# The compression MLP of a sparse-attention branch, moved between the projections of a delta rule and spread over four column quarters of TensorE

## The chip, the core and the metric

The kernel runs on one core of a Trainium2 chip. It is one program with five in-order engines: TensorE (PE, and PEld for its weight loads), VectorE (DVE), ScalarE (ACT), GpSimd (POOL) and SyncE (SP), whose queue issues nearly all transfers. The metric is device time in microseconds. Before the change three runs gave 2414.8, 2419.28 and 2424.24 us, so the median is 2419.28 us.

## The reference

One decoder layer on 256 tokens of width 2048: SwiGLU, a mixer with two branches, a second SwiGLU, final RMSNorm. The change concerns the mixer. One input projection feeds a gated delta rule with 8 heads of 128 and a sparse attention whose keys and values are also compressed: 15 blocks of 32 tokens (stride 16) for each of 2 key/value groups, so 30 positions, each flattened to 4096 numbers and put through a small MLP. It is done once for keys and once for values:

```python
def _compress(x, pos, w1, b1, w2):
    b, s, g, d = x.shape
    r = CMP_BLOCK // CMP_STRIDE
    n_cmp = s // CMP_STRIDE - r + 1
    xs = x.reshape(b, s // CMP_STRIDE, CMP_STRIDE, g, d)
    blocks = jnp.concatenate([xs[:, j:j + n_cmp] for j in range(r)], axis=2)
    blocks = blocks + pos[None, None, :, None, :]
    flat = blocks.transpose(0, 1, 3, 2, 4).reshape(b, n_cmp, g, CMP_BLOCK * d)
    return jax.nn.silu(flat @ w1 + b1) @ w2
...
    kc, vc, ks, vs, kw, vw = [t.reshape(b, s, NSA_KV_HEADS, NSA_HEAD_DIM) for t in jnp.split(nkv, 6, axis=-1)]
...
    kcmp = _compress(kc, pos_k, k_w1, k_b1, k_w2)
    vcmp = _compress(vc, pos_v, v_w1, v_b1, v_w2)
```

The attention's first step (`compressed`, L989) needs `kcmp`; the delta rule needs nothing of it.

## The kernel before

A projection is `win(c)` (L608): 128 output columns for all 256 tokens. Its weights come as two blocks of 128 x 1024 floats (512 KB) into the ring `raw` of six slots (`wload`, L157). ScalarE rounds a block to `whi` (L171), VectorE makes the rest `wlo` (L172), three buffers each, and TensorE then does 16 pairs of matmuls (`product`, L181 and L183). `both` (L207, L210) empties the bank. After each projection `ada(tk())` may put in a unit that streams two 512 KB blocks of `ada_w` through the same ring and adds them up on VectorE (L234); `paces` gives 4 units to the first 27 projections of the mixer and then one to each of the next 20. Every eighth unit ends in transposes (L240).

The delta rule runs in four groups of two heads (the loop of L913 to L918): `gdn_qkv` projects and convolves q, k and v of the next two heads while `gdn_group` works on the last two; its chain of small matmuls on TensorE (L730 to L895, among them the 32 x 32 steps L803 and L813) waits in turn on VectorE and ScalarE. `gdn_out` adds two gate projections. A scheduler lays the recorded work out, engine by engine, in one fixed order, so what stands in a queue behind a waiting instruction waits too.

The compression follows the last group (L932 to L972). Four projections give `cat`. For keys (b = 0) and then values (b = 1), `G` holds the 30 positions for each of the 32 offsets (L946, one buffer), and 32 matmuls of 128 x 30 against 128 x 128 weights (L952) add up in one bank of the `mm` ring, all of them in TensorE's first 32 columns. In float32 each such matmul is two passes. The eight 512 KB blocks of `cw1` lie in the `raw` ring until TensorE has read them. A tail of bias, tanh (L955 to L958), transpose (L960), copy (L962) and a second small matmul (L966 or L970) gives `kcmp` and `vcmp`. `attend_in` (8 projections) and `attend` follow for each of the two groups.

Of the kernel before, what the change touches and what calls it, by code (L numbers as in the profile page):

```python
# [18 lines left out]
F32 = mybir.dt.float32  # L19
# [3 lines left out]
AF = mybir.ActivationFunctionType  # L23
OP = mybir.AluOpType
# [3 lines left out]
P = 128  # L28
S = 256
# [26 lines left out]
NB = 15  # L56
# [9 lines left out]
C_I32 = C_CMP + 32  # L66
# [41 lines left out]
def trunk(tc, a, out, stage=99, dbg=None):  # L108
    nc = tc.nc
    ctx = ExitStack()  # L110
    with ctx:
# [30 lines left out]
        V = {}  # L142
# [53 lines left out]
        def tmpc():  # L196
            return tmp("tc", 2)
# [53 lines left out]
        def ada(n):  # L251
            for _ in range(n):
                if ada_q:
                    ada_unit(*ada_q.pop(0))
# [349 lines left out]
        with ExitStack() as mx:  # L604
            mp = mx.enter_context(tc.tile_pool(name="mp", bufs=1))
            tk = paces((4, 31 - 2 * NE), (20, 20), (24, 36))

            def win(c):  # L608
                if c in done:
                    return done.pop(c)  # L610
                ps = proj(a["win"][c], hT)
                ada(tk())
                return ps

            def one(tag="q", bufs=12):
# [88 lines left out]
            def gdn_qkv(h0):  # L704
                q, k, v = [], [], []
                for lst, w0, c0 in ((k, W_GK, 8), (q, W_GQ, 0), (v, W_GV, 16)):
                    for h in (h0, h0 + 1):
                        lst.append(conv_silu(win(w0 + h), c0 + h))
                        if h0 == 0 and len(q) + len(k) + len(v) == SCA:
                            scalars()  # L710
                return q, k, v
# [188 lines left out]
            def gdn_out(h0, oT):  # L900
                for i in range(2):
                    h = h0 + i
                    zg = both(win(W_GZ + h))
                    th = tmp()
                    nc.scalar.activation(th, zg, AF.Tanh, scale=0.5)
                    sg = mp.tile([P, S], F32, tag="sg", name="sg", bufs=1)
                    nc.vector.scalar_tensor_tensor(sg, th, 1.0, zg, op0=OP.add, op1=OP.mult)
                    sv = sg.rearrange("p (a b) -> p a b", a=2)
                    nc.vector.tensor_mul(sv, sv, v4(oT)[:, :, i])
                    oA[h] = big("oA", 8, (P, 2, S), F32R)  # L910
                    split(oA[h], sg)

            qkv = gdn_qkv(0)  # L913
            for h0 in (0, 2, 4, 6):
                oT = gdn_group(h0, *qkv)
                if h0 < 6:
                    qkv = gdn_qkv(h0 + 2)
                gdn_out(h0, oT)  # L918

            def rope(x, o, pt, tr):
# [5 lines left out]
                nc.vector.tensor_mul(o[:32], x[:32], cf[:32, C_COS:C_COS + S])  # L928
                nc.vector.tensor_add(o[:32], o[:32], t[:32])
                return o  # L930

            cat = [mp.tile([P, 2, S], F32, tag="cat", name="cat", bufs=2) for _ in range(2)]  # L932
            for b in range(2):
                for g in range(2):
                    both(win(W_KV + 2 * b + g), cat[b][:, g])
            kcmp = mp.tile([P, 2 * NB], F32, name="kcmp")
            vcmp = mp.tile([16, 2, P], F32, name="vcmp")
            b1 = mp.tile([2 * NB, 2, P], F32, name="b1")
            nc.scalar.dma_start(b1, bass.AP(tensor=a["cb1"].tensor, offset=a["cb1"].offset,
                                            ap=[[0, 2 * NB], [P, 2], [1, P]]))  # L940
            for b in range(2):
                G = mp.tile([P, 32, 2, NB], F32, tag="G", name="G", bufs=1)
                for g in range(2):
                    src = cat[b][:, g]
                    blocks = bass.AP(tensor=src.tensor, offset=src.offset, ap=[list(src.ap[0]), [1, 32], [16, NB]])
                    nc.vector.tensor_add(G[:, :, g], blocks,  # L946
                                         V["pos"][:, 32 * b:32 * b + 32].unsqueeze(2).to_broadcast([P, 32, NB]))
                ph = mmtile()
                for q, (raw, n) in enumerate(wload(a["cw1"][b], 32)):
                    for j in range(n):  # L950
                        jj = 8 * q + j
                        nc.tensor.matmul(ph[:2 * NB, :P], G[:, jj].rearrange("p a b -> p (a b)"), raw[:, j],  # L952
                                         start=(jj == 0), stop=(jj == 31))
                hid = mp.tile([2 * NB, P], F32, tag="hid", name="hid", bufs=1)
                nc.vector.tensor_add(hid, ph[:2 * NB, :P], b1[:, b])  # L955
                th = tmpc()[:2 * NB, :P]
                nc.scalar.activation(th, hid, AF.Tanh, scale=0.5)
                nc.vector.scalar_tensor_tensor(hid, th, 1.0, hid, op0=OP.add, op1=OP.mult)  # L958
                pt = ftile()
                nc.tensor.transpose(pt[:, :2 * NB], hid, ident[:2 * NB, :2 * NB])  # L960
                hT2 = tmpc()[:, :2 * NB]
                nc.scalar.activation(hT2, pt[:, :2 * NB], AF.Copy, scale=0.5)  # L962
                w2 = V["w2"][:, b * P:(b + 1) * P]
                pc = ftile()
                if b == 0:
                    nc.tensor.matmul(pc[:, :2 * NB], w2, hT2, start=True, stop=True)  # L966
                    nc.vector.tensor_copy(kcmp, pc[:, :2 * NB])
                else:
                    for g in range(2):
                        nc.tensor.matmul(pc[:NB, g * P:(g + 1) * P], hT2[:, g * NB:(g + 1) * NB], w2,  # L970
                                         start=True, stop=True)
                    nc.vector.tensor_copy(vcmp[:NB], pc[:NB, :2 * P].rearrange("p (a b) -> p a b", a=2))  # L972

            PR = [("pr", 2), ("pr", 2), ("G", 1)]

# [184 lines left out]


VEC = [("ada_b", 144), ("n1", 16), ("nm", 16), ("n2", 16), ("nf", 16), ("conv", 96), ("alog", 1), ("dtb", 1),
       ("gnw", 1), ("pos", 64), ("w2", 256)]


def layout(i):
    f = lambda n: np.asarray(i[n])
    cols = lambda v: np.ascontiguousarray(v.reshape(-1, P).T)

    def tiles(w):  # L1170
        k, n = w.shape
        return np.ascontiguousarray(w.reshape(k // P, P, n // P, P).transpose(2, 1, 0, 3))

    o = {}
    o["xT"] = np.ascontiguousarray(f("x")[0].T.reshape(KT, P, S).transpose(1, 0, 2))
# [19 lines left out]
    v = {"ada_b": cols(f("ada_b")[0]), "n1": cols(f("ffn1_norm")[0]), "nm": cols(f("mix_norm")[0]),  # L1195
         "n2": cols(f("ffn2_norm")[0]), "nf": cols(f("final_norm")),
         "conv": f("gdn_conv_w")[0].reshape(24, P, 4).transpose(1, 0, 2).reshape(P, 96),
         "alog": row32(f("gdn_a_log")[0]), "dtb": row32(f("gdn_dt_bias")[0]),
         "gnw": f("gdn_norm_w")[0].reshape(P, 1),
         "pos": np.concatenate([f("cmp_pos_k")[0].T, f("cmp_pos_v")[0].T], axis=1),  # L1200
         "w2": np.concatenate([f("cmp_k_w2")[0], f("cmp_v_w2")[0]], axis=1)}
    o["vec"] = np.ascontiguousarray(np.concatenate([v[n] for n, _ in VEC], axis=1))
    o["cw1"] = np.ascontiguousarray(np.stack([f("cmp_k_w1")[0], f("cmp_v_w1")[0]]).reshape(2, 32, P, P)
                                    .transpose(0, 2, 1, 3))
    o["cb1"] = np.ascontiguousarray(np.stack([f("cmp_k_b1")[0], f("cmp_v_b1")[0]]))
    o["consts"] = float_consts()
    o["masks"] = block_masks()
    return o
# [17 lines left out]
```

## Time and profile before

| | us |
|---|---|
| median of three runs | 2419.28 |
| the profiled execution | 2422.17 |
| its span | 2420.4 |
| PE busy | 2349.7 |
| DVE busy | 1789.9 |
| ACT busy | 1130.5 |

The rows below come from that one execution, whose granted TensorE clock was 0.99 on the mean; 1.8 us of its time lie outside its span. Times in rows are microseconds from the start of the span. A PE row counts a matmul as busy until its modelled end, so rows that follow each other overlap, and the cost of one in a stream is the distance of its start from the next start. "[1.70 <-DVE hid L958]" is idle time of the engine before the row, and what ended it.

### The profile page before, as it was taken

Reading aid. Unit: us, or ns where it says so; the run is one execution under the profiler, and the core shown is the slowest. Engines: PE = TensorE matmul, PEld = TensorE weight load, DVE = VectorE, ACT = ScalarE, POOL = GpSimd, SP = SyncE. Lnnn points to the kernel's source line nnn. Section 1 sums busy time; section 2 is a strip of 40 time slices with the busy share of each in tenths; the row PEclk is TensorE's granted clock in tenths of the full one; section 3 lists DMA queues with packets and bytes.
Section 4 is the critical chain, followed back from the end, with each engine's and each line's share of the span. In section 5 each row is a group of like instructions: output and inputs, shape, how many; then the busy total and the mean of one; then the engine's idle time right before and its main releaser. Section 6 shows DMA issues by size and latency. Waiting matters only on the chain.

```text
span 2420.4 us, 39304 instructions
## 1 busy us (share of the span) xinstructions
PE 2349.7 (97%) x15308; PEld 2062.4 (85%) x15308; DVE 1789.9 (74%) x2641; ACT 1130.5 (47%) x1780; POOL 1.2 (0%) x6
## 2 busy tenths in 40 slices
PE   7999999999999999999999999999999999999997
PEld 6999988888888988887888878889888888888886
DVE  6899878778887887785887677878666666555555
ACT  3533544334444565543544444556444444344443
POOL 0000000000000000000000000000000000000000
PEclk7999999999999999999999999999999999999999
DMA  9998688888996644566776887576777776665663
GB/s 326 317 312 306 199 282 302 280 274 296 315 303 218 220 159 142 157 204 211 262 256 214 289 275 257 188 236 201 238 240 236 231 235 204 189 191 185 183 184 121
DMA packets 182872, 571.08 MB, mean 236 GB/s; under 512 B 18047, under 2 KB 18333, under 8 KB 182685
## 3 DMA queue, kind: packets, MB, share of 16 engines
q1 hardware_dynamic: 181920, 566.43, 71.5%
q8 instruction: 120, 1.97, 0.3%
q10 hardware_dynamic: 765, 2.14, 0.2%
q14 instruction: 67, 0.55, 0.1%
HBM read 564.30 MB, written 4.19 MB: 235 GB/s over the span
## 4 chain that ended last, share of the span: by engine, by line
PE 74%; DMA 11%; DVE 9%; issue 3%; ACT 1%; DVEq 0%; ACTq 0%; SPq 0%
PE mm L181 39%; PE mm L183 20%; DMA adaraw<-in_ada_w_dram 8%; PE mm L348 8%; DVE wlo L172 3%; DMA sada<-in_ada_w_dram 2%; PE c L348 2%; DVE acc L234 1%; DVE wlo L343 1%; DMA raw<-in_win_dram 1%; DVE sacc L443 1%; ACT whi L171 0%; PE f L240 0%; PE c L1026 0%; PE c L813 0%
## 5 line engine op out<-in xcount | busy, mean ns | idle before, releaser
L181 PE MATMUL mm<-hpair,whi 128*128 128x512 f32 x3536 | 1260.9, 398 | 1.1 <-ACT t L203 1.1
L172 DVE TENSOR_TENSOR wlo<-raw,whi 128x1024 fp32r<-128x1024 f32 (+1 forms) x666 | 793.0, 1196 | 350.9 <-ACT whi L171 349.3
L171 ACT ACTIVATE whi<-raw 128x1024 fp32r<-128x1024 f32 (+1 forms) x666 | 689.3, 1037 | 726.2 <-PE mm L181 420.9
L183 PE MATMUL mm<-hpair,wlo 128*128 128x256 f32 x3536 | 1004.7, 284 | 18.6 <-DVE wlo L172 18.4
L181 PEld LDWEIGHTS mm<-hpair,whi 128*128 128x128 f32 x3536 | 665.5, 188 | 160.1 <-issue 1.8
L183 PEld LDWEIGHTS mm<-hpair,wlo 128*128 128x128 f32 x3536 | 668.2, 189 | 30.3 <-DVE wlo L172 24.6
L181 PE MATMUL mm<-apair,whi 128*128 128x512 f32 x1408 | 497.7, 397 | 0.0
L183 PE MATMUL mm<-apair,wlo 128*128 128x256 f32 x1408 | 397.3, 282 | 5.5 <-DVE wlo L172 5.5
L234 DVE SCALAR_TENSOR_TENSOR acc<-adaraw,cact,acc 128x1024 f32<-128x1024 f32 x210 | 268.8, 1280 | 133.8 <-DMA adaraw<-in_ada_w_dram 132.8
L181 PEld LDWEIGHTS mm<-apair,whi 128*128 128x128 f32 x1408 | 264.3, 188 | 64.0
L183 PEld LDWEIGHTS mm<-apair,wlo 128*128 128x128 f32 x1408 | 265.4, 188 | 8.6 <-DVE wlo L172 8.4
L348 PE MATMUL mm<-hpair,whi 128*128 128x256 f32 x1472 | 265.7, 283 | 2.4 <-ACT hpair L309 1.8
L348 PEld LDWEIGHTS mm<-hpair,whi 128*128 128x128 f32 x1472 | 228.1, 190 | 3.0 <-ACT hpair L309 1.9
L348 PE MATMUL mm<-hpair,wlo 128*128 128x256 f32 x736 | 209.3, 285 | 1.4 <-DVE wlo L343 1.4
L342 ACT ACTIVATE whi<-raw 128x1024 fp32r<-128x1024 f32 x112 | 118.4, 1059 | 141.3 <-DMA raw<-in_w1gu_dram 56.4
L343 DVE TENSOR_TENSOR wlo<-raw,whi 128x1024 fp32r<-128x1024 f32 x112 | 136.5, 1222 | 30.2 <-ACT whi L342 30.1
L348 PEld LDWEIGHTS mm<-hpair,wlo 128*128 128x128 f32 x736 | 139.8, 190 | 2.6 <-DVE wlo L343 2.2
L207 ACT ACTIVATE t<-mm 128x256 f32<-128x256 f32 x237 | 86.9, 367 | 17.7 <-PE mm L183 17.6
L210 DVE TENSOR_TENSOR t<-mm,t 128x256 f32<-128x256 f32 x193 | 80.7, 418 | 2.5 <-ACT t L207 2.4
L443 DVE SCALAR_TENSOR_TENSOR sacc<-sada,cact,sacc 128x1024 f32<-128x1024 f32 x57 | 73.0, 1281 | 8.0 <-DMA sada<-in_ada_w_dram 7.3
L532 ACT ACTIVATE t<-t 128x256 f32<-128x256 f32 x63 | 26.3, 418 | 100.5 <-DVE t L210 100.2
L546 DVE SCALAR_TENSOR_TENSOR xT<-mm,g,xT 128x256 f32<-128x256 f32 x128 | 61.7, 482 | 7.7 <-PE mm L183 5.6
(373 smaller groups left out, 1586.7 us busy)
## 6 DMA issues: line engine op xcount, KB each, us to landing
adaraw<-in_ada_w_dram SPq DMA_DIRECT2D x224, 512.0 KB, 5.1
raw<-in_w2gu_dram SPq DMA_DIRECT2D x180, 512.0 KB, 4.7
raw<-in_w1gu_dram SPq DMA_DIRECT2D x176, 512.0 KB, 5.9
raw<-in_win_dram SPq DMA_DIRECT2D x158, 512.0 KB, 5.0
sada<-in_ada_w_dram SPq DMA_DIRECT2D x64, 512.0 KB, 6.4
raw<-in_w1d_dram SPq DMA_DIRECT2D x64, 512.0 KB, 4.6
raw<-in_w2d_dram SPq DMA_DIRECT2D x64, 512.0 KB, 3.5
raw<-in_wup_dram SPq DMA_DIRECT2D x32, 512.0 KB, 4.6
```

The costliest lines, as they stand in the source:

```text
L171: nc.scalar.activation(hi[:, :n], raw[:, :n], AF.Copy)
L172: nc.vector.tensor_sub(lo[:, :n], raw[:, :n], hi[:, :n])
L181: nc.tensor.matmul(ps[:, :], hi, pairs[k][:, :, :].rearrange("p a b -> p (a b)"), start=(k == 0), stop=False, skip_group_check=True)
L183: nc.tensor.matmul(ps[:, S:2 * S], lo, pairs[k][:, 0, :], start=False, stop=(k == n - 1), skip_group_check=True)
L207: nc.scalar.activation(t, ps[:, S:2 * S], AF.Copy)
L210: nc.vector.tensor_add(o, ps[:, :S], t)
L234: nc.vector.scalar_tensor_tensor(acc, raw, cact[:, kt:kt + 1], acc, op0=OP.mult, op1=OP.add)
L342: nc.scalar.activation(hi, raw, AF.Copy)
L343: nc.vector.tensor_sub(lo, raw, hi)
L348: nc.tensor.matmul(ps[:, w], l[:, w, k], h[:, r], start=(first and w == k == x == 0), stop=(last and k == kb - 1 and x == 2), skip_group_c ...
L443: nc.vector.scalar_tensor_tensor(acc, raw, c, acc, op0=OP.mult, op1=OP.add)
L546: nc.vector.scalar_tensor_tensor(xT[:, d], pd[:, j * S:(j + 1) * S], g05[:, d:d + 1], xT[:, d], op0=OP.mult, op1=OP.add)
```

## The change

`compress` is now a generator. It is made after the first two heads' q, k and v are projected, and each later `win` call of the delta rule takes one step of it: a `cat` projection, or one block of `cw1` with its 8 matmuls, or a tail. Seven steps for the keys and seven for the values make 14, and 26 `win` calls follow. `G` has 32 columns, the last two zero. Matmul j goes to the quarter j % 4 of the columns, into 32 partitions of its own in a bank `f`. The tail copies the 128 x 128 partial sums (`hs`), adds the four quarters by a matmul with four stacked identities (which also turns the result round), and takes the bias from a packed vector instead of a DMA of its own.

```diff
-            def win(c):
+            beside = []
+
+            def win(c, step=True):
                 if c in done:
                     return done.pop(c)
                 ps = proj(a["win"][c], hT)
                 ada(tk())
+                if step and beside:
+                    next(beside[0], None)
                 return ps
...
+            def compress():
+                for b in range(2):
+                    cat = mp.tile([P, 2, S], F32, tag="cat", name="cat", bufs=2)
+                    for g in range(2):
+                        both(win(W_KV + 2 * b + g, False), cat[:, g])
+                        yield
+                    G = mp.tile([P, 32, 32], F32, tag="G", name="G", bufs=1)
+                    nc.gpsimd.memset(G[:, :, 2 * NB:], 0.0)
+                    for g in range(2):
+                        src = cat[:, g]
...
+                        nc.vector.tensor_add(G[:, :, g * NB:(g + 1) * NB], blocks,
...
+                    ph = ftile()
+                    for r in range(4):
+                        (raw, _), = wload(a["cw1"][b][:, 8 * r:8 * r + 8], 8)
+                        for j in range(8):
+                            jj = 8 * r + j
+                            q = slice(32 * (j % 4), 32 * (j % 4) + 32)
+                            nc.tensor.matmul(ph[q, :P], G[:, jj], raw[:, j], start=(jj < 4), stop=(jj >= 28),
+                                             skip_group_check=True)
+                        yield
+                    hs = mp.tile([P, P], F32, tag="hs", name="hs", bufs=1)
+                    nc.scalar.activation(hs, ph[:, :P], AF.Copy)
+                    pt = ftile()
+                    nc.tensor.matmul(pt[:, :2 * NB], hs, cf[:, C_I32:C_I32 + 2 * NB], start=True, stop=True)
+                    hid = mp.tile([P, 2 * NB], F32, tag="hid", name="hid", bufs=1)
+                    nc.scalar.activation(hid, pt[:, :2 * NB], AF.Identity, bias=V["b1"][:, b:b + 1])
+                    th = tmpc()[:, :2 * NB]
+                    nc.scalar.activation(th, hid, AF.Tanh, scale=0.5)
+                    hT2 = tmpc()[:, :2 * NB]
+                    nc.vector.scalar_tensor_tensor(hT2, th, 1.0, hid, op0=OP.add, op1=OP.mult)
...
             qkv = gdn_qkv(0)
+            beside.append(compress())
             for h0 in (0, 2, 4, 6):
                 oT = gdn_group(h0, *qkv)
                 if h0 < 6:
                     qkv = gdn_qkv(h0 + 2)
                 gdn_out(h0, oT)
+            for _ in beside.pop():
+                pass
...
-            nc.scalar.dma_start(b1, bass.AP(tensor=a["cb1"].tensor, offset=a["cb1"].offset,
-                                            ap=[[0, 2 * NB], [P, 2], [1, P]]))
...
-                ph = mmtile()
-                for q, (raw, n) in enumerate(wload(a["cw1"][b], 32)):
-                    for j in range(n):
-                        jj = 8 * q + j
-                        nc.tensor.matmul(ph[:2 * NB, :P], G[:, jj].rearrange("p a b -> p (a b)"), raw[:, j],
-                                         start=(jj == 0), stop=(jj == 31))
...
```

On TensorE, at the end of the last group of heads, the order before was this (L952 are the compression's matmuls, L240 the transposes of an `ada` unit, L895 the end of the delta rule's chain, L960 and L966 the tail):

```order
L240 MATMUL f<-cf,acc 128x128 x4
L952 MATMUL mm<-raw,G 30x128 x6
L240 MATMUL f<-cf,acc 128x128 x4
L952 MATMUL mm<-raw,G 30x128 x10
L895 MATMUL c<-cf,o 128x128 x4
L952 MATMUL mm<-raw,G 30x128 x16
L960 MATMUL f<-cf,hid 128x30
L966 MATMUL f<-tc,vec 128x30
L952 MATMUL mm<-raw,G 30x128 x32
L181 MATMUL mm<-hpair,whi 128x512
```

All 64 matmuls stood here, with the tail of the keys directly between those of the keys and those of the values. Now they stand in eights; the first eight (L941, in the first group of heads, where L807, L817 and L837 are steps of the delta rule) are these:

```order
L181 MATMUL mm<-hpair,whi 128x512
L807 MATMUL c<-tb,N 32x32 x8
L183 MATMUL mm<-hpair,wlo 128x256
L181 MATMUL mm<-hpair,whi 128x512
L183 MATMUL mm<-hpair,wlo 128x256
L817 MATMUL c<-zc,q_9247 32x32
L941 MATMUL f<-raw,G 32x128
L817 MATMUL c<-zc,q_9247 32x32 x7
L941 MATMUL f<-raw,G 32x128 x7
L181 MATMUL mm<-hpair,whi 128x512
L183 MATMUL mm<-hpair,wlo 128x256
```

The other seven bursts are whole and have a projection's matmuls on both sides; the tail's L947 stands 32 matmuls behind its last burst, and L957 13 matmuls behind L947. On SP, whose queue issues the blocks, this stood before around the compression:

```order
L230 DMA adaraw<-in_ada_w_dram 128x1024 x2
L162 DMA raw<-in_cw_dram 128x1024 x8
L162 DMA raw<-in_win_dram 128x1024 x2
L230 DMA adaraw<-in_ada_w_dram 128x1024 x2
L162 DMA raw<-in_win_dram 128x1024 x2
```

and this stands now, in the first two groups of heads:

```order
L162 DMA raw<-in_win_dram 128x1024 x12
L162 DMA raw<-in_cw_dram 128x1024
L162 DMA raw<-in_win_dram 128x1024 x2
L230 DMA adaraw<-in_ada_w_dram 128x1024 x2
L162 DMA raw<-in_cw_dram 128x1024
L162 DMA raw<-in_win_dram 128x1024 x2
L162 DMA raw<-in_cw_dram 128x1024
L162 DMA raw<-in_win_dram 128x1024 x2
L162 DMA raw<-in_cw_dram 128x1024
```

The eight blocks no longer follow each other: at least two blocks of a projection lie between any two of them.

## Rows read from the trace of the kernel before

**Rows 1.** The page, part 1: busy time, share and instructions of each engine.

```profile
PE 2349.7 (97%) x15308; PEld 2062.4 (85%) x15308; DVE 1789.9 (74%) x2641; ACT 1130.5 (47%) x1780; POOL 1.2 (0%) x6
```

**Rows 2.** Windows: the four head groups, the stretch to attention, and one inside attention.

```profile
core 0: us, PE busy (x) PEld busy (x) DVE busy (x) ACT busy (x) POOL busy (x), PEclk, DMA share, GB/s
871.10:931.70 60.60, 59.45 (x623) 50.18 (x622) 50.49 (x124) 35.91 (x88) 0.00 (x0) 0.99 0.45 142
931.70:994.90 63.20, 62.35 (x638) 52.22 (x637) 50.73 (x119) 34.58 (x84) 0.00 (x0) 1.00 0.47 151
994.90:1061.40 66.50, 65.08 (x656) 54.92 (x655) 53.08 (x123) 36.51 (x93) 0.00 (x0) 1.00 0.53 166
1061.40:1111.90 50.50, 47.67 (x558) 39.39 (x557) 38.24 (x93) 17.37 (x38) 0.00 (x0) 1.00 0.55 178
1111.90:1180.80 68.90, 64.60 (x398) 54.73 (x396) 51.93 (x67) 26.12 (x39) 0.00 (x0) 0.98 0.87 299
...
1200.00:1220.00 20.00, 20.00 (x116) 16.53 (x115) 19.23 (x43) 11.04 (x30) 0.00 (x0) 1.00 0.71 231
```

**Rows 3.** Timeline (start, us, engine, line): a projection's pairs, first and eighth L181.

```profile
1085.60 0.39 PE L181 MATMUL mm<-hpair,whi 128*128 128x512 f32 x1
...
1088.05 0.40 PE L181 MATMUL mm<-hpair,whi 128*128 128x512 f32 x1
```

**Rows 4.** Groups by line, TensorE, 1100 to 1140: busy, mean ns, idle before.

```profile
L952 PE MATMUL mm<-raw,G 128*30 128x128 f32 x128 | 14.7, 273 | 0.0
...
L970 PE MATMUL f<-vec,tc 128*15 128x128 f32 x4 | 0.9, 364 | 0.9 <-ACT tc L962 0.9
...
L960 PE MATMUL f<-cf,hid 30*128 30x30 f32 x2 | 0.5, 228 | 3.1 <-DVE hid L958 3.1
L966 PE MATMUL f<-tc,vec 128*128 128x30 f32 x2 | 0.4, 284 | 0.3 <-ACT tc L962 0.3
```

**Rows 5.** Timeline: two runs of L952, the first with its entry wait.

```profile
1113.25 3.41 PEld L952 LDWEIGHTS mm<-raw,G 128*30 128x30 f32 x32 [0.17 <-issue]
...
1119.47 7.17 PE L952 MATMUL mm<-raw,G 128*30 128x128 f32 x64
```

**Rows 6.** Timeline: 32 x 32 steps on four tiles and on two.

```profile
1088.74 0.34 PEld L803 LDWEIGHTS c<-tb,N 32*32 32x32 f32 x32 [0.26 <-issue]
1088.74 0.45 PE L803 MATMUL c<-tb,N 32*32 32x32 f32 x32
...
1092.71 0.44 PE L803 MATMUL c<-tb,N 32*32 32x32 f32 x16
```

**Rows 7.** Groups by line, 845 to 1320, the same steps: busy, mean ns, idle before.

```profile
L803 PE MATMUL c<-tb,N 32*32 32x32 f32 x576 | 9.1, 194 | 4.4 <-DVE tb L794 4.4
```

**Rows 8.** Timeline: four pairs after the values' tail, first and fifth L181.

```profile
1132.84 0.80 PE L181 MATMUL mm<-hpair,whi 128*128 128x512 f32 x1
...
1135.57 0.44 PE L181 MATMUL mm<-hpair,whi 128*128 128x512 f32 x1
```

**Rows 9.** Windows: the tail of the values, and those four pairs.

```profile
1126.60:1132.80 6.20, 3.90 (x20) 2.59 (x19) 2.63 (x4) 1.45 (x3) 0.00 (x0) 0.95 0.89 347
1132.80:1135.60 2.80, 2.80 (x10) 2.38 (x10) 1.46 (x3) 1.06 (x1) 0.00 (x0) 0.50 1.00 377
```

**Rows 10.** Groups by line, VectorE, 845 to 1320: busy, mean ns, idle before.

```profile
L172 DVE TENSOR_TENSOR wlo<-raw,whi 128x1024 fp32r<-128x1024 f32 x112 | 136.1, 1219 | 30.7 <-ACT whi L171 30.0
L234 DVE SCALAR_TENSOR_TENSOR acc<-adaraw,cact,acc 128x1024 f32<-128x1024 f32 x56 | 71.4, 1274 | 9.9 <-DMA adaraw<-in_ada_w_dram 9.8
...
L946 DVE TENSOR_TENSOR G<-cat,vec 128x480 f32<-128x480 f32 x4 | 3.9, 972 | 0.0
```

**Rows 11.** Waits of SP's queue, 1060 to 1181: us, times, longest.

```profile
SPq L162 <- PE mm L952: 21.1, 5, 16.1
```

**Rows 12.** The page, part 6: transfers of a projection's weights, median to landing.

```profile
raw<-in_win_dram SPq DMA_DIRECT2D x158, 512.0 KB, 5.0
```

More of the change, by code (lines that the diff above doesn't have):

```diff
@@ L911, in gdn_out @@
                     split(oA[h], sg)
+            kcmp = mp.tile([P, 2 * NB], F32, name="kcmp")
+            vcmp = mp.tile([16, 2, P], F32, name="vcmp")
+            def compress():
[8 more added lines that the diff above has]
+                        src = cat[:, g]
+                        blocks = bass.AP(tensor=src.tensor, offset=src.offset, ap=[list(src.ap[0]), [1, 32], [16, NB]])
+                        nc.vector.tensor_add(G[:, :, g * NB:(g + 1) * NB], blocks,
+                                             V["pos"][:, 32 * b:32 * b + 32].unsqueeze(2).to_broadcast([P, 32, NB]))
+                    ph = ftile()
[17 more added lines that the diff above has]
+                    nc.vector.scalar_tensor_tensor(hT2, th, 1.0, hid, op0=OP.add, op1=OP.mult)
+                    w2 = V["w2"][:, b * P:(b + 1) * P]
+                    pc = ftile()
+                    if b == 0:
+                        nc.tensor.matmul(pc[:, :2 * NB], w2, hT2, start=True, stop=True)
+                        nc.scalar.activation(kcmp, pc[:, :2 * NB], AF.Copy, scale=0.5)
+                    else:
+                        for g in range(2):
+                            nc.tensor.matmul(pc[:NB, g * P:(g + 1) * P], hT2[:, g * NB:(g + 1) * NB], w2,
+                                             start=True, stop=True)
+                        nc.scalar.activation(vcmp[:NB], pc[:NB, :2 * P].rearrange("p (a b) -> p a b", a=2), AF.Copy,
+                                             scale=0.5)
+                    yield
@@ L930, in rope @@
                 return o
[L932 to L938, printed above, removed]
-            nc.scalar.dma_start(b1, bass.AP(tensor=a["cb1"].tensor, offset=a["cb1"].offset,
-                                            ap=[[0, 2 * NB], [P, 2], [1, P]]))
@@ L941, in trunk @@
[L941 to L947, printed above, removed]
-                ph = mmtile()
-                for q, (raw, n) in enumerate(wload(a["cw1"][b], 32)):
-                    for j in range(n):
-                        jj = 8 * q + j
-                        nc.tensor.matmul(ph[:2 * NB, :P], G[:, jj].rearrange("p a b -> p (a b)"), raw[:, j],
-                                         start=(jj == 0), stop=(jj == 31))
[L954 to L972, printed above, removed]
@@ L1162 @@
 VEC = [("ada_b", 144), ("n1", 16), ("nm", 16), ("n2", 16), ("nf", 16), ("conv", 96), ("alog", 1), ("dtb", 1),
-       ("gnw", 1), ("pos", 64), ("w2", 256)]
+       ("gnw", 1), ("pos", 64), ("w2", 256), ("b1", 2)]
 def layout(i):
@@ L1200, in layout @@
          "pos": np.concatenate([f("cmp_pos_k")[0].T, f("cmp_pos_v")[0].T], axis=1),
-         "w2": np.concatenate([f("cmp_k_w2")[0], f("cmp_v_w2")[0]], axis=1)}
+         "w2": np.concatenate([f("cmp_k_w2")[0], f("cmp_v_w2")[0]], axis=1),
+         "b1": np.stack([f("cmp_k_b1")[0], f("cmp_v_b1")[0]], axis=1)}
     o["vec"] = np.ascontiguousarray(np.concatenate([v[n] for n, _ in VEC], axis=1))
@@ L1204, in layout @@
                                     .transpose(0, 2, 1, 3))
-    o["cb1"] = np.ascontiguousarray(np.stack([f("cmp_k_b1")[0], f("cmp_v_b1")[0]]))
     o["consts"] = float_consts()
```

## Prediction

> **What bounds the kernel now.** I read the page's busy shares first. TensorE is busy 2349.7 us of 2420.4, every other engine 74% or less [rows 1]. So a change gains only what it takes out of TensorE's stream or its waits, and a delay costs only where it reaches that stream. Next come windows over the mixer, cut where VectorE starts each group of heads (871.1, 931.7, 994.9, 1061.4), where it ends the last (1111.9) and where attention starts (1180.8) [rows 2]. The reader is to see that TensorE is nearly full in the first three, that its gaps grow from 1061 on (2.8 and 4.3 us outside its busy time), and that VectorE stands at 75 to 83% throughout. The compression lies at the end, from 1108 to 1133. A projection's price is read from its pairs: seven in 2.45 us, 0.35 a pair, so 16 take 5.6 us [rows 3].
>
> **What is removed.** The 64 matmuls L952 are 128 passes and fill 14.7 us of TensorE with nothing beside them on that engine [rows 4]. In the longer run 64 passes take 7.17 us, the last of them 0.27, so one pass starts (7.17 - 0.27) / 63 = 0.11 us after the other [rows 4, 5]. A run begins with an entry wait of about 0.17 us [rows 5]; at four runs, as the order has them, I count three of these outside the busy time, 0.5, and put the whole at 15.2 us.
>
> Between the runs TensorE waits for the tails: 3.1 us at L960, 0.3 at L966 and 0.9 at L970, together 4.3 [rows 4]. These waits arise because the tail's links stand in TensorE's queue with few or no matmuls between them. The four pairs after the values' tail then take 2.73 us instead of 4 x 0.35 = 1.40, a loss of 1.3 [rows 3, 8]; the granted clock of that stretch is 0.50, so 1.2 GHz, behind 6.2 us in which TensorE was busy for 3.9 [rows 9]. Waits and slow pairs make 5.6 us. What is late next there is the projections and attention's first steps, which need nothing of the tails for eight projections more.
>
> **What is added.** The same 128 passes, now in eight bursts of 16, four streams of four passes each. The trace of before has no burst whose tiles share all rows and differ in columns alone, so the price is bounded from two sides. As one stream a burst takes 15 x 0.11 + 0.27 + 0.17 = 2.1 us, eight of them 16.7. Wholly side by side it takes 3 x 0.11 + 0.27 + 0.17 = 0.77, eight of them 6.2. The nearest rows are the delta rule's 32 x 32 steps: 32 passes on four tiles take 0.45 us, 16 passes on two tiles 0.44 [rows 6]. With 0.19 for the last one [rows 7] that is 8 ns from start to start on four tiles and 17 on two: twice the tiles, half the distance. Those tiles differ in rows and columns both. I take 6.2, since it is the only behaviour that any row of side-by-side tiles shows, and the upper end stays in the range. TensorE then gains 15.2 - 6.2 = 9.0 us.
>
> Each of these steps begins with a wait of its own, 0.26 us in that row [rows 6]; if the bursts pay that instead of 0.17, the eight cost 0.7 more. The Trainium skill (TensorEngine Tiling (Array Packing), Key Properties) says that a change of tiling mode drains the engine, a rule against cutting four runs into eight. The entry waits agree with it; by the rule the sum changes by no more than those entry waits, which are in it.
>
> **What is moved.** Four projections (4 x 5.6 us of TensorE) come from the last group of heads into the first two; attention's projections take their place beside the last chain, so TensorE's amount of work stays. The four additions into `G`, 0.97 us each on VectorE [rows 10], stand well ahead of their bursts in VectorE's order, the eight transfers of `cw1` are the same bytes, and the removed bias transfer was nobody's wait. All these I cost at nothing, with the projections between as cover; without it, an addition would cost its 0.97.
>
> New waits: a tail now has 32 matmuls before its first link and 13 before its second. 32 matmuls are 5.6 us, for one ScalarE copy; 13 are 2.3 us, for two ScalarE steps and a VectorE step that may stand behind one `wlo` of 1.22 [rows 10]. Behind a waiting link the projection's other matmuls are queued. I take 0.5 for both tails; the bounds are nothing and the 4.3 of before.
>
> VectorE loses its slack at the end. The mixer's 28th to 47th projections carry one `ada` unit each, and these now begin four projections earlier in the delta rule. Counted in the order of VectorE's instructions, the third group has 3 more of its 1.27 us additions, the fourth 9 more, with 6 more `wlo` of 1.22 and without two additions into `G` [rows 10]. So the third rises from 53.1 to 56.9 us and the fourth from 38.2 to 38.2 + 11.4 + 7.3 - 1.9 = 55.0. TensorE has 65.1 there and 47.7 - 34 x 0.11 + 3 x 5.6 = 60.8 [rows 2]. VectorE is thus at 87 and 90% of TensorE, more than in any head group of before, but it was at 96% in a window inside attention with TensorE full [rows 2]. I take 1.0 us of new waits, between nothing and the 9.0 of the second rival.
>
> **The sum**: -9.0 - 5.6 + 0.5 + 1.0 = -13.1 us. Against the profiled execution, 2422.17, that is 2409.1. That execution lies 2.9 above the median of the three runs; against the median, 2419.28, it is 2406.2, and 2406 is the forecast.
>
> **Rivals.** First: the quarters don't run side by side. All four take the same 128 rows, and what the 32 x 32 steps show is for tiles that share none. Then the eight bursts cost 16.7, TensorE loses 1.5, and the sum is +1.5 - 5.6 + 1.5 = -2.6: 2417. Halfway, two at a time, a burst takes 7 x 0.11 + 0.27 + 0.17 = 1.2, eight 9.7, and the sum is -5.5 - 5.6 + 1.5 = -9.6: 2410. Against it: the weight load of the next pass of L952 shared all its rows with the pass in flight and still did not lengthen the 0.11. The Trainium skill (TensorE: Matmul & The Clock Gate, Part 3) states that a weight load overlaps matmuls in flight only where row groups differ, which would give this rival; the 0.11 of L952 does not bear that out. The same section gives 2.38 times for three column tiles; as an estimate from that page, four would give 3.2 times, 0.11 / 3.2 a pass, about 0.9 us more than I take over all eight bursts (16 x 0.11 / 3.2 = 0.55 in place of 4 x 0.11 = 0.44).
>
> Second: VectorE becomes the bound of the third and fourth groups. If it can be filled only to the 83% of the fullest head group (50.49 of 60.60) [rows 2], those stretches take 56.9 / 0.83 = 68.6 and 55.0 / 0.83 = 66.3, which is 3.5 and 5.5 over TensorE's 65.1 and 60.8. With 9.0 in place of 1.0 the sum is -5.1: 2414. For it speaks that small steps of the chain wait in VectorE's queue behind 1.2 us blocks (4.4 us before L803 [rows 7]); against it the 96% in attention.
>
> Third, the slower one: the ring. A `cw1` block keeps its slot until TensorE's burst has read it, while a projection's block is free once split. Before, SP stood 21.1 us in five waits on L952, 16.1 in the longest [rows 11]. TensorE runs up to three split blocks behind, 3 x 8 x 0.35 = 8.4 us, and a block lands 5.0 us after its issue [rows 12]. If SP stood for the whole 8.4 at each of the eight blocks, each next block would be ready 8.4 + 5.0 - 8.4 = 5.0 us too late: 8 x 5.0 = 40, less 13.1, gives +27, 2446. It decides from 25 us of such lateness on, 3.1 a block. Against it: five slots remain, 5 x 2.8 = 14 us of TensorE's work, before SP must come back to the kept one, and the order has no two `cw1` blocks in a row.
>
> **How the numbers follow.** Forecast 0.60, with its own range 2400 to 2412; one stream 0.13; two at a time 0.08; VectorE 0.12; the ring 0.07. About 0.5% is what a measurement of this kernel can tell from no change: 12.1 us, so faster means below 2407.2. The forecast lies just beyond that: two thirds of its chance, 0.40, and 0.02 of the two-at-a-time case are faster. The ring's 0.07 is slower; the rest, 0.51, is the same. The range goes from 2397 (-9.0 - 5.6, no new wait, and the 4.4 of L803 gone with the new filling, -19, with 3 for the scatter of a median of runs that differ by 9) to 2418 (one stream); it leaves out the ring and a little on each side.
>
> **What would show it.** Each step has its place in the new profile: a burst of L941 about 0.6 us long with passes 0.03 apart on the mean (wrong at 0.11); L947, L957 and L961 waiting less than 0.5 together (wrong at some us); no stretch at 0.50 after 1100; the first head group's window longer by about three projections and the second's by one, and attention's first row at about 1168 instead of 1181. VectorE over 90% with gaps on TensorE in the last group would be the second rival, SP's waits on L941 with ScalarE waiting for landings the third. The forecast is wrong if attention starts less than 8 or more than 18 us earlier.

## The result, and the profile after

The changed kernel takes 2404.33 us (median of four runs, 2402.11 to 2405.89); the kernel before took 2418.92 beside it. That is 14.6 us or 0.6% less: the ratio is 0.9940, its 95% interval 0.9926 to 0.9953. The forecast was 2406, with a range of 2397 to 2418. One execution of those reported below, of the kernel with the quarters at the old place, took 5831.41 us, and no ratio counts it.

First the page's busy times, part 1, of the changed kernel:

```profile
PE 2333.8 (97%) x15310; PEld 2048.3 (85%) x15310; DVE 1786.4 (74%) x2637; ACT 1130.7 (47%) x1784; POOL 1.5 (0%) x8
```

TensorE is busy 15.9 us less than in [rows 1] with two instructions more, and the busy time of VectorE, ScalarE and GpSimd has moved by no more than 3.5. The profiled execution, 2402.11 us, is the fastest of its four and its span is 20.1 us shorter than that of before. Not all of this belongs to the change. VectorE begins the first group of heads at 866.9 instead of 871.1, and in the eight traces of the experiments below the same row starts between 867.8 and 872.6, so these 4.2 us are put down to scatter. From there to attention it is 294.0 us instead of 309.7, so the change is worth 15.7 here. The windows of the changed kernel, cut at the same places as [rows 2] (columns as there):

```profile
866.90:948.70 81.80, 80.22 (x790) 67.09 (x790) 63.78 (x140) 44.08 (x103) 0.16 (x1) 0.99 0.54 175
948.70:1020.40 71.70, 70.92 (x738) 58.71 (x737) 54.51 (x124) 37.50 (x89) 0.00 (x0) 1.00 0.57 186
1020.40:1084.00 63.60, 61.91 (x638) 52.15 (x638) 56.05 (x124) 34.23 (x82) 0.00 (x0) 1.00 0.61 189
1084.00:1144.80 60.80, 60.53 (x625) 50.25 (x623) 56.30 (x114) 28.26 (x63) 0.00 (x0) 1.00 0.80 262
1144.80:1160.90 16.10, 15.43 (x94) 13.13 (x93) 13.61 (x24) 7.56 (x12) 0.00 (x0) 1.00 0.83 292
sum 294.00, PE 289.01 PEld 241.33 DVE 244.25 ACT 151.63 POOL 0.16; mean PE 57.80 PEld 48.27 DVE 48.85 ACT 30.33 POOL 0.03
```

The rows are to be read in two halves. TensorE's busy time over the stretch is 289.0, against 299.15 for the five windows of [rows 2] together: -10.1. The time in which it was not busy is 294.0 - 289.0 = 5.0, against 309.7 - 299.15 = 10.55: -5.6. The first window is 21 us longer than the first of before and the second 8.5 longer, since the four projections, the bursts and the tails now lie there; the stretch behind the last group falls from 68.9 to 16.1.

The busy half is the bursts. A group by line, TensorE, changed kernel, 895 to 1015, answers to [rows 4]:

```profile
L941 PE MATMUL f<-raw,G 128*32 128x128 f32 x128 | 5.6, 279 | 0.0
L947 PE MATMUL f<-cf,hs 128*128 128x30 f32 x4 | 0.6, 234 | 0.0
L961 PE MATMUL f<-vec,tc 128*15 128x128 f32 x4 | 0.6, 272 | 0.1
L957 PE MATMUL f<-tc,vec 128*128 128x30 f32 x2 | 0.4, 274 | 0.0
```

The same 128 passes take 5.6 us instead of 14.7, though one pass is as long as ever (279 ns). The last column shows the other half: the tails' links L947, L957 and L961 together wait 0.1. One burst in TensorE's timeline:

```profile
913.10 0.28 PE L183 MATMUL mm<-hpair,wlo 128*128 128x256 f32 x1
913.31 0.65 PE L941 MATMUL f<-raw,G 128*32 128x128 f32 x16
913.89 0.50 PE L181 MATMUL mm<-hpair,whi 128*128 128x512 f32 x1
```

Between two pairs without a burst, L181 starts 0.12 after L183; here it starts 0.79 after it. So a burst costs the stream 0.67 us, its entry included. In the records its 16 starts lie within 0.37 us, in rounds of four with 7 ns from start to start; eight bursts at this price come to 5.4 (the first is cut in two by steps of the chain, and the fifth stands right behind one). The waits of TensorE from 865 to 1181, changed kernel (total, times, longest):

```profile
PE c L807 <- DVE tb L798: 2.0, 3, 0.8
PE c L817 <- issue: 1.1, 1, 1.1
PE c L899 <- DVE o L896: 0.7, 1, 0.7
PE mm L181 <- ACT t L203: 0.6, 1, 0.6
PE c L807 <- DVE modc L242: 0.3, 1, 0.3
```

L807 is the line that was L803 [rows 7]: its 4.4 us of waits have become 2.0, with 0.3 more that end with `modc`. In the kernel before, 871 to 1181, the waits that neither the tails [rows 4] nor L803 had were these:

```profile
PE c L895 <- DVE o L892: 0.8, 3, 0.4
PE c L813 <- issue: 0.6, 1, 0.6
PE mm L181 <- ACT t L203: 0.4, 1, 0.4
```

### The profile page after: what moved, and what is told of

Same layout as the page of the kernel before. It is cut to its first block, busy times and chain, and to the rows that moved or that the text cites. A ratio compares the mean times of both kernels' runs of the same rounds, so it can differ in the third digit from the quotient of the medians.

```text
span 2400.3 us, 39307 instructions
## 1 busy us (share of the span) xinstructions
PE 2333.8 (97%) x15310; PEld 2048.3 (85%) x15310; DVE 1786.4 (74%) x2637; ACT 1130.7 (47%) x1784; POOL 1.5 (0%) x8
## 4 chain that ended last, share of the span: by engine, by line
PE 79%; DMA 9%; DVE 8%; issue 2%; ACT 1%; DVEq 0%; SPq 0%; ACTq 0%
PE mm L181 41%; PE mm L183 21%; PE mm L348 9%; DMA adaraw<-in_ada_w_dram 8%; DVE wlo L172 3%; PE c L348 2%; DMA sada<-in_ada_w_dram 1%; DVE acc L234 1%; DVE sacc L443 1%; DVE wlo L343 1%; DMA raw<-in_win_dram 0%; PE c L1041 0%; PE f L240 0%; ACT whi L171 0%; PE c L817 0%
## 5 line engine op out<-in xcount | busy, mean ns | idle before, releaser
L181 PE MATMUL mm<-hpair,whi 128*128 128x512 f32 x3536 | 1259.5, 398 | 1.4 <-ACT t L203 1.4
L183 PE MATMUL mm<-hpair,wlo 128*128 128x256 f32 x3536 | 1003.7, 284 | 21.3 <-DVE wlo L172 21.1
L181 PEld LDWEIGHTS mm<-hpair,whi 128*128 128x128 f32 x3536 | 665.1, 188 | 159.4 <-issue 2.8
L183 PEld LDWEIGHTS mm<-hpair,wlo 128*128 128x128 f32 x3536 | 668.3, 189 | 33.3 <-DVE wlo L172 28.1
L181 PE MATMUL mm<-apair,whi 128*128 128x512 f32 x1408 | 498.1, 397 | 0.0
L183 PE MATMUL mm<-apair,wlo 128*128 128x256 f32 x1408 | 397.2, 282 | 3.3 <-DVE wlo L172 3.1
L181 PEld LDWEIGHTS mm<-apair,whi 128*128 128x128 f32 x1408 | 264.3, 188 | 64.6
L183 PEld LDWEIGHTS mm<-apair,wlo 128*128 128x128 f32 x1408 | 265.4, 188 | 5.5 <-DVE wlo L172 5.5
```

The costliest lines, as they stand in the source:

```text
L181: nc.tensor.matmul(ps[:, :], hi, pairs[k][:, :, :].rearrange("p a b -> p (a b)"), start=(k == 0), stop=False, skip_group_check=True)
L183: nc.tensor.matmul(ps[:, S:2 * S], lo, pairs[k][:, 0, :], start=False, stop=(k == n - 1), skip_group_check=True)
```

## The experiments

Each kernel is timed beside the kernel before on the same chip. Beside the first four that kernel took 2421.63 us, beside the last four 2419.40. The changed kernel itself was run only with the first four; the last four are set against it by their ratios. Its own ratio was 0.9940 in the first comparison and 0.9922 here, so differences of that size between the two sets say nothing.

**The changed kernel once more**, for comparison with the next three.

> The changed kernel once more, on the chip of the three kernels below, so that they are compared with it and not only with the kernel before. Every theory expects 14.6 us less than before (2418.92 to 2404.33 in the first runs), within 3.

Measured: 2403.35 us, ratio 0.9922 (0.9906 to 0.9937), 18.3 us faster. The gain differs by 4 us from the first comparison, and the intervals overlap.

**Dealt out, but all in one quarter.** The bursts keep their places and lose the spreading; the scheduler cuts two of them into more pieces.

```diff
-                            q = slice(32 * (j % 4), 32 * (j % 4) + 32)
-                            nc.tensor.matmul(ph[q, :P], G[:, jj], raw[:, j], start=(jj < 4), stop=(jj >= 28),
+                            q = slice(0, 32)
+                            nc.tensor.matmul(ph[q, :P], G[:, jj], raw[:, j], start=(jj == 0), stop=(jj == 31),
...
-                    nc.scalar.activation(hs, ph[:, :P], AF.Copy)
+                    nc.scalar.activation(hs[:32], ph[:32, :P], AF.Copy)
...
-                    nc.tensor.matmul(pt[:, :2 * NB], hs, cf[:, C_I32:C_I32 + 2 * NB], start=True, stop=True)
+                    nc.tensor.matmul(pt[:, :2 * NB], hs[:32], cf[:32, C_I32:C_I32 + 2 * NB], start=True, stop=True)
```

> Dealt out as in the changed kernel, but all 64 matmuls in the first quarter of the columns, one sum of 32 partitions, so the four quarters need no adding up. Theory (the quarters' passes run side by side and TensorE is the bound beside the delta rule): a burst goes from about 0.67 us to 16 x 0.11 + 0.25 = 2.0, eight bursts cost 10.6 more, so 10 us slower than the changed kernel, about 4 faster than the kernel before. Rival (TensorE has slack in the delta rule's groups, which hides a longer burst): at most 3 us slower than the changed kernel.

Measured: 2411.79 us, ratio 0.9955 (0.9939 to 0.9972): 8.4 slower than the changed kernel and still 9.8 faster than before. The loss is about as large as expected; what is left of the gain is larger, since dealing out took more waits than those of the tails. The same burst, timeline of TensorE:

```profile
915.49 0.28 PE L183 MATMUL mm<-hpair,wlo 128*128 128x256 f32 x1
915.70 1.94 PE L941 MATMUL f<-raw,G 128*32 128x128 f32 x16
917.57 0.50 PE L181 MATMUL mm<-hpair,whi 128*128 128x512 f32 x1
```

From L183 to L181 it is 2.08 us, 1.96 for the burst. The quarters take 8 x (1.96 - 0.67) = 10.3 us off the bursts by these rows; by time they are worth 8.4, and a table below shows where a part is lost again.

**In quarters, but at the old place**, all of it behind the last group of heads.

```diff
-            beside.append(compress())
...
-            for _ in beside.pop():
+            for _ in compress():
```

> The four quarters, but the compression in its old place, all after the last group of heads; nothing dealt out. Theory (the two parts add up: 9.6 us from the quarters, 5.6 from the waits and slow pairs of the tails, which stay here): 9 to 10 us faster than before, 5 slower than the changed kernel. Rival (eight 512 KB blocks in a row come no faster than one stream reads them, so quarters alone gain nothing in the old place): within 3 us of the kernel before.

Measured: 2412.41 us, ratio 0.9959 (0.9943 to 0.9974): 9.1 slower than the changed kernel, 9.2 faster than before. The tails do not wait here either, so dealing out was not needed to take their waits away: the scheduler now laid 3 to 8 other matmuls between their links. The tail itself is written anew in both single changes (a sum in bank `f`, no bias transfer of its own); no run has the new tail alone, so what its form gives is not measured. Yet TensorE waits as long as before, elsewhere. Its waits from 866 to 1165 in this kernel:

```profile
PE c L807 <- DVE tb L798: 5.0, 5, 2.5
PE c L899 <- DVE o L896: 1.3, 4, 0.6
PE mm L183 <- DVE wlo L172: 1.2, 3, 0.8
PE mm L181 <- ACT t L203: 1.1, 1, 1.1
PE f L981 <- DVE t L210: 1.1, 2, 0.9
PE mm L181 <- ACT whi L171: 0.6, 1, 0.6
```

What is new is waiting for `wlo` and `whi`, the split weights: 1.8 us, less than half of the 4.3 that the tails gave up. The rest is spread over L981 (1.1) and longer waits at L807, L899 and L203. ScalarE's waits from 1060 to 1165 show that the weights landed late:

```profile
ACT whi L171 <- DMA raw<-in_win_dram: 17.3, 11, 2.7
```

In the kernel before, that wait is 4.8 us between 871 and 1181; in the changed kernel there is none. Why the weights are late stands in SP's queue. The blocks of `cw1` do not come in one row here: the scheduler laid them in two fours, the first issued at 1063.8 to 1071.1 and the second at 1093.7 to 1098.7. From 1050 to 1161 SP stands for the bursts that read them:

```profile
SPq L230 <- PE f L941: 5.3, 1, 5.3
SPq L162 <- PE f L941: 3.5, 1, 3.5
```

The longer of the two ends when TensorE has begun to read the second four, at 1113.26. These are the timelines of SP, ScalarE and TensorE:

```profile
1108.27 6.02 SPq L230 DMA_DIRECT2D adaraw<-in_ada_w_dram  x2
1114.40 0.84 SPq L162 DMA_DIRECT2D raw<-in_win_dram  x2
...
1119.99 1.06 ACT L171 ACTIVATE whi<-raw 128x1024 fp32r<-128x1024 f32 x1 [0.63 <-DMA raw<-in_win_dram]
...
1121.10 0.50 PE L181 MATMUL mm<-hpair,whi 128*128 128x512 f32 x1 [0.61 <-ACT whi L171]
```

Between its two `ada` transfers SP stands for a slot, then issues the projection's blocks, and ScalarE starts on the first as it lands, 5.6 us after its issue. The wait for `wlo` that follows on TensorE is 0.8. While SP stands the DMA engines have little to do, and afterwards they are full:

```profile
1108.00:1114.40 6.40, 6.40 (x78) 5.58 (x80) 5.19 (x11) 2.55 (x5) 0.00 (x0) 1.00 0.30 84
...
1120.00:1140.00 20.00, 18.45 (x98) 14.40 (x98) 17.01 (x20) 9.44 (x13) 0.00 (x0) 1.00 0.97 365
```

So the kept slots of the ring, the prediction's third rival, are at work here: the two waits on TensorE that follow from the longer stand are 1.4 of the 1.8 us. A slow stretch also came back elsewhere. This window holds TensorE's longest wait, 2.5 us at L807, and its granted clock is below the 1.00 that the kernel before has in the same window:

```profile
1060.00:1080.00 20.00, 17.55 (x241) 14.53 (x239) 16.77 (x43) 6.82 (x13) 0.00 (x0) 0.91 0.68 212
```

The two single changes and the full one can be put side by side over one stretch with the same work: from the 1441st matmul L183, in the first group of heads, to the 3201st, behind attention. One window each, of before:

```profile
874.20:1696.80 822.60, 798.55 (x5793) 681.99 (x5792) 647.22 (x1181) 403.11 (x763) 0.00 (x0) 1.00 0.66 219
```

of the kernel that is dealt out on one quarter:

```profile
871.70:1686.30 814.60, 798.12 (x5796) 680.59 (x5794) 646.42 (x1177) 402.72 (x767) 0.16 (x1) 1.00 0.66 221
```

of the quarters at the old place:

```profile
870.00:1685.00 815.00, 789.66 (x5797) 672.34 (x5795) 647.90 (x1177) 404.65 (x767) 0.16 (x1) 1.00 0.66 221
```

and of the changed kernel, run again:

```profile
871.70:1678.60 806.90, 788.36 (x5796) 670.96 (x5795) 644.82 (x1177) 402.49 (x767) 0.16 (x1) 1.00 0.67 223
```

| | stretch | TensorE busy | not busy |
|---|---|---|---|
| before | 822.6 | 798.6 | 24.0 |
| dealt out only | -8.0 | -0.4 | -7.6 |
| quarters only | -7.6 | -8.9 | +1.3 |
| both | -15.7 | -10.2 | -5.5 |

Dealing out takes waits and next to no busy time, quarters take busy time and no waits, and the two add up: 8.0 + 7.6 = 15.6 of 15.7. By time it is 9.8 + 9.2 = 19.0 of 18.3. Each row is one execution. In the first trace of the changed kernel the stretch is again 806.9 us, but 786.8 of it busy and 20.1 not, so the two columns on the right scatter by 1.6, and that the sum meets within 0.1 is luck. On top of dealing out the quarters take 9.8 of busy time and give 2.1 back in waits, 7.7 in all, which is near the 8.4 by time.

**Neighbours in one quarter.** If a burst were fast only because each pass goes to another quarter than the pass before it, this order would be slow.

```diff
-                            q = slice(32 * (j % 4), 32 * (j % 4) + 32)
-                            nc.tensor.matmul(ph[q, :P], G[:, jj], raw[:, j], start=(jj < 4), stop=(jj >= 28),
+                            q = slice(32 * (j // 2), 32 * (j // 2) + 32)
+                            nc.tensor.matmul(ph[q, :P], G[:, jj], raw[:, j], start=(r == 0 and j % 2 == 0), stop=(r == 3 and j % 2 == 1),
```

> As the changed kernel, but two matmuls that follow each other go to the same quarter (j // 2 in place of j % 4), so four passes in a row share a tile. Theory (each quarter has a queue of its own in effect, and the order inside a burst is free): the burst stays at about 0.65 us and the time that of the changed kernel within 2 us. Rival (matmuls start in order, so a pass behind one of its own quarter holds up the rest): at most two quarters at once, a burst of 1.2 us, 8 x 0.5 = 4 us slower than the changed kernel.

Measured: 2402.62 us, ratio 0.9914 (0.9894 to 0.9934), as the changed kernel. The burst, timeline of TensorE:

```profile
917.20 0.28 PE L183 MATMUL mm<-hpair,wlo 128*128 128x256 f32 x1
917.41 0.66 PE L941 MATMUL f<-raw,G 128*32 128x128 f32 x16
918.00 0.50 PE L181 MATMUL mm<-hpair,whi 128*128 128x512 f32 x1
```

0.80 from L183 to L181, against 0.79. The order inside a burst makes no difference that counts.

**The `ada` units later**, so that VectorE has less to add up in the third and fourth groups. If it were the bound there, this would gain.

```diff
-            tk = paces((4, 31 - 2 * NE), (20, 20), (24, 36))
+            tk = paces((4, 35 - 2 * NE), (20, 20), (24, 36))
```

> The changed kernel with the dense run of ada units begun four projections later, so that it starts where it did before the change, counted in what the delta rule does; the last two groups of heads lose four units, 4 x 2.55 = 10 us of VectorE. Theory (VectorE at 93% of the last group's window costs TensorE nothing): within 2 us of the changed kernel. Rival (VectorE binds the third and fourth groups): 3 to 8 us faster than the changed kernel.

Measured: 2404.66 us, ratio 0.9939 (0.9916 to 0.9962), which cannot be told from the changed kernel. The changed kernel's own windows say why: in the fourth group VectorE is busy 56.30 of 60.80 us, 93%, while TensorE is busy 60.53. In the kernel with later `ada` VectorE is busy only 51.3 of the third group's 63.4 us and 47.6 of the fourth's 58.1, 81 and 82%, but TensorE is idle for 2.7 us in the two groups together, against 2.0 and 2.4 in the two traces of the changed kernel. And in this window of the changed kernel both are full:

```profile
1068.00:1088.00 20.00, 20.00 (x124) 17.60 (x124) 20.00 (x34) 13.43 (x37) 0.00 (x0) 1.00 0.86 278
```

**Begun one group of heads later.**

```diff
-            beside.append(compress())
...
+                if h0 == 2:
+                    beside.append(compress())
```

> The changed kernel with the dealing out begun one group of heads later, so that it fills the second and third groups' projections. Theory (TensorE is full in every group, so the place is free as long as projections stand between): within 2 us of the changed kernel. Rival (the gain hangs on the first groups, where VectorE has slack): 3 us slower or more.

Measured: 2405.67 us, ratio 0.9941 (0.9921 to 0.9962), 1 us from the kernel of the last experiment and inside its interval. Its tails wait 2.0 us at L957 and L961 in the profiled execution, more than the changed kernel's 0.1, but by time neither this kernel and the one before it nor this and the changed one can be told apart; a loss of 3 us, as the rival had it, is neither shown nor excluded.

**Four bursts of 32 passes** instead of eight of 16.

```diff
-                        yield
+                        if r % 2:
+                            yield
```

> The changed kernel with two blocks of cw1 and 16 matmuls in a step: four bursts in place of eight. Theory (each burst pays its switch, 0.25 us of its 0.67): TensorE busy about 1 us less and the time 1 us less, which a median can hardly tell, so the trace decides. Rival (a kept slot of the ring holds up the projections' blocks, and now two are kept at once): slower by 2 us or more, with ScalarE waiting for landings beside the bursts.

Measured: 2406.34 us, ratio 0.9944 (0.9923 to 0.9965), so no gain. The bursts themselves did get cheaper. Groups by line of this kernel, 865 to 1180:

```profile
L941 PE MATMUL f<-raw,G 128*32 128x128 f32 x128 | 4.7, 276 | 0.0
```

That is 0.9 us less than the changed kernel's 5.6. Elsewhere one wait was longer than any of the changed kernel's; TensorE's timeline of this kernel:

```profile
969.02 0.50 PE L807 MATMUL c<-tb,N 32*32 32x32 f32 x21 [3.60 <-DVE tb L798]
```

A first 32 x 32 step stood in TensorE's queue 3.6 us before VectorE had its input ready. Behind it the granted clock was 0.50 (1.2 GHz):

```profile
969.00:973.00 4.00, 3.98 (x73) 3.34 (x74) 3.08 (x5) 1.64 (x3) 0.00 (x0) 0.50 0.83 289
```

In the profiled execution, 2410.46 us and the slowest of the six, wait and slow stretch outweighed the 0.9. That the fewer, larger steps of the compression brought this wait about, by moving the work around the delta rule's steps, is likely but was not tried; nor is it known whether the other five executions had it. The rival's sign is hardly there: in the profiled execution ScalarE waits once for a landing, 1.5 us. The difference of the times, 1.7 us from the kernel with later `ada`, lies within the intervals: a gain of 1 us is not to be had in this way, and a loss is not shown.

**Two quarters.**

```diff
-                            q = slice(32 * (j % 4), 32 * (j % 4) + 32)
-                            nc.tensor.matmul(ph[q, :P], G[:, jj], raw[:, j], start=(jj < 4), stop=(jj >= 28),
+                            q = slice(32 * (j % 2), 32 * (j % 2) + 32)
+                            nc.tensor.matmul(ph[q, :P], G[:, jj], raw[:, j], start=(jj < 2), stop=(jj >= 30),
...
-                    nc.scalar.activation(hs, ph[:, :P], AF.Copy)
+                    nc.scalar.activation(hs[:64], ph[:64, :P], AF.Copy)
...
-                    nc.tensor.matmul(pt[:, :2 * NB], hs, cf[:, C_I32:C_I32 + 2 * NB], start=True, stop=True)
+                    nc.tensor.matmul(pt[:, :2 * NB], hs[:64], cf[:64, C_I32:C_I32 + 2 * NB], start=True, stop=True)
```

> The changed kernel with two quarters of the columns in place of four, to see how the passes scale. Theory (time of a burst goes with the passes of one quarter): a start every 0.055 us on the mean, a burst of 1.1 us, eight bursts 3.5 us more than with four quarters and 7 less than with one: 3 to 4 us slower than the changed kernel. Rival (the passes overlap only in pairs, or the engine orders them otherwise): the time of one quarter or of four.

Measured: 2406.27 us, ratio 0.9948 (0.9929 to 0.9967). Its burst, timeline of TensorE:

```profile
918.22 0.28 PE L183 MATMUL mm<-hpair,wlo 128*128 128x256 f32 x1
918.43 1.07 PE L941 MATMUL f<-raw,G 128*32 128x128 f32 x16
919.43 0.50 PE L181 MATMUL mm<-hpair,whi 128*128 128x512 f32 x1
```

1.21 from L183 to L181, so 1.09 for the burst, between 1.96 on one quarter and 0.67 on four. Eight of them cost 8 x (1.09 - 0.67) = 3.4 us more than on four. The times alone would not show it, since the interval is as wide; the rows do.

## Why the prediction was right, step by step

**The quarters, -9.0.** The prediction took 0.77 a burst, as if four streams ran wholly side by side, on the strength of the 32 x 32 steps [rows 6], which differ in rows too. That this carries over to tiles with the same rows was assumed there, and it came true. A burst costs 0.67, and on one quarter 1.96 where the prediction had 2.1. So the difference is 10.3 by the two kernels' rows, 9.1 by the groups by line (14.7 to 5.6), and 8.4 by time. The first two rivals, one stream and two at a time, are out: rows of 1.94 and 1.07 us are what they would look like, and the changed kernel's is 0.65.

**Tails and slow pairs, -5.6.** The 4.3 us of waits [rows 4] are 0.1. Every window of the changed kernel above from 948.7 on has a granted clock of 1.00, so the pairs at 0.50 [rows 9] are gone too. The reason was only half right. The prediction has the waits go because matmuls stand between the links. That can be had at the old place too, but there other waits took their place, those for late weights among them. It is dealing out that lowers the sum of TensorE's waits.

**New waits, +0.5 and +1.0.** Neither came as such. The tails wait 0.1 in place of 0.5. VectorE rose in the third group to 56.05 us and in the fourth to 56.30, where 56.9 and 55.0 were foreseen, and so to 88 and 93% of the stretch; yet TensorE's waits fell. The 4.4 at the 32 x 32 steps [rows 7] became 2.0 (2.9 in the second trace), which the prediction had only in the low end of its range. In the kernel before all of them stand ahead of a group's first step. In the last group it was 2.19 before and is 0.27 now:

```profile
1075.54 0.45 PE L803 MATMUL c<-tb,N 32*32 32x32 f32 x32 [2.19 <-DVE tb L794]
...
1098.71 0.45 PE L807 MATMUL c<-tb,N 32*32 32x32 f32 x32 [0.27 <-DVE modc L242]
```

Counted in the records, 110 pairs of projections stood between the third group's last such step (L803, now L807) and this one in the kernel before, and 120 in the changed kernel, ten more at 0.35 us each [rows 3]. That is 3.5 us of work ahead of a wait of 2.2. The two single changes agree: dealt out on one quarter it is 120 pairs and 0.28 us, quarters at the old place 110 pairs and 2.46 us. But the count alone does not decide. With `ada` later it is 130 pairs and 1.16 us, so what stands in VectorE's queue counts as well, and that the ten pairs are the cause is argued and not shown. Other small waits grew by 1.0 in all, at L817 most.

By the rows of the first trace the sum is -9.1 (bursts) - 1.3 (slow pairs) - 4.2 (tails) - 2.4 (L807) + 1.0 = -16.0, against 15.7 measured over the stretch and -13.1 predicted. The term that was off is the new waits: +1.5 was foreseen and -2.4 + 1.0 = -1.4 came, 2.9 us that the times alone could not show. The two comparisons gave 14.6 and 18.3 us, so that 2404.33 lies within 2 us of the forecast is in part luck.

**The signs.** The burst (0.65 us) and the tails (0.1) came as foretold, and up to attention no window after 1100 is below a granted clock of 1.00; one behind attention's start, 1424 to 1428, has 0.57, as one in the kernel before has, 1463 to 1467. One sign speaks against the forecast by its letter: it called itself wrong if attention started more than 18 us earlier, and attention starts at 1160.9, 19.9 earlier. The sign was badly set, since it counts from the start of the span and takes in the scatter ahead of the first group, 4.2 us here. Counted from that group it is 15.7, and 16.4 in the second trace, where attention starts at 1162.8.

**VectorE as the bound** (2414) is out: at 93% and at 100% beside a nearly full TensorE no cost is seen, and with less of its work there TensorE is idle for as long.

**The ring** (2446) is out as a cost, though the wait that it needs is there. SP's queue, changed kernel, 866 to 1161:

```profile
SPq L162 <- PE f L941: 15.3, 7, 4.1
```

SP stood seven times for a burst, 2.2 us on the mean and 4.1 at most, where the prediction let this rival decide from 3.1 of lateness a block. But standing is not lateness: ScalarE never waits for a landing in that stretch, so the other slots held what it needed. At the old place they did not: there SP stood 8.8 us in two waits, and TensorE waited 1.4 us for weights that were issued too late.

## What to carry to other kernels

Small float32 matmuls that use 32 columns of TensorE can be given to its four column quarters, in either order tried here, and summed by one matmul with stacked identities: here 16 passes then took 0.67 us instead of 1.96. At the old place this gained half of what was to be had, since other waits took the place of the tails', in part for weights that SP could issue only when TensorE had read the kept slots of the ring. Dealt out between projections, with at least two other blocks between any two, it lowered the sum of the waits too; that work put ahead of the chain's first steps did this is likely. Busy time and waits of the same stretch, read apart, show which part of a change brought what; a 1 us term is better read from rows than from times that scatter by 4, though idle time in rows of one execution scatters as well, here by 1.6.

## What the runs showed of the hardware

The four column quarters share all 128 rows and still run fully side by side. In the records a round of four passes starts 0.11 us after the round before it (0.13 after the first), as a single pass does on one quarter; for 16 passes the rows have 1.94 us on one quarter, 1.07 on two and 0.65 on four. The Trainium skill (TensorE: Matmul & The Clock Gate, Part 3) says that a weight load overlaps matmuls in flight only where the row groups differ; these rows do not agree, since here all row groups are the same and the 16 loads, 0.38 us in the row below, lie inside the passes' 0.65. The same section also has loads pulled ahead into a background weight buffer, with which the rows would agree; no run shows which it is. For three column tiles and 512 columns streamed it gives 2.38 times; here four, with 128 columns, gave 1.96 / 0.67 = 2.9 times with the entry, and near 4 without it.

The entry shows in the weight loads' timeline of the changed kernel, at the burst shown above:

```profile
913.31 0.38 PEld L941 LDWEIGHTS f<-raw,G 128*32 128x32 f32 x16 [0.26 <-issue]
```

Weight loads stand idle for 0.26 us ahead of the burst, as they did for the 32 x 32 steps [rows 6]. The Trainium skill (TensorEngine Tiling (Array Packing), Key Properties) says that a change of tiling mode drains the engine; these rows agree with it, but do not show what the 0.26 us go into.

TensorE's granted clock fell to 0.50 behind the wait of 3.6 us in the kernel with four bursts, and below 1.00 in the window with a wait of 2.5 us at the old place. It did not behind the wait of 2.19 us at the same step in the kernel before, where the window 1060 to 1080 has 1.00.
